# A chunked delta-rule scan in fp32: both directions in lockstep, transposes between the inversion's products

## The chip, the cores and the metric

The kernel runs on one core of a Trainium2 chip, as one program. The metric is the time of one execution on the device in microseconds, less is better. Arithmetic is fp32; the engines named below are PE (matrix products), PEld (its weight loads), DVE (vector), ACT (scalar), POOL (GpSimd) and SP, whose queue issues the DMAs.

## The reference, cut to what matters

A two-layer backbone: an RWKV-7 mixer, an MLP, a Fourier mixer, an MLP, over 1024 latent tokens of 1024 channels with a prefix of 256 context tokens. The change touches the mixer's scan, which runs for 16 heads of 64 channels and for two directions over 256 + 1024 tokens:

```python
def step(s, inp):
    w_t, k_t, v_t, a_t, b_t = inp[:5]
    sa = jnp.einsum('bhvk,bhk->bhv', s, a_t)
    s = s * w_t[:, :, None, :] + sa[..., None] * b_t[:, :, None, :] + v_t[..., None] * k_t[:, :, None, :]
    y = jnp.einsum('bhvk,bhk->bhv', s, inp[5]) if with_out else None
    return s, y
```

`s` is a 64x64 state per head and direction. Direction 1 runs over the tokens in reverse. The context's outputs are not needed, its final states are where the latent scans start.

## The kernel before, in words

A first phase makes the streams of the scan and writes them to DRAM, scaled by running products of the decays. The scan then takes 64 tokens at a time: 20 steps, the first 4 of context, each for both directions `d`. Within a step the 64 updates are solved at once, as a triangular system: the strictly triangular matrix of a head is cut into two halves of 32 tokens, the diagonal 32x32 blocks are inverted, and the second half is solved after the first. Two heads share a tile (`hh`, on partitions 0 to 63 and 64 to 127), eight pairs `q` lie side by side.

One step in `scan_step`, by the lines of the profile: `mms` (L945) multiplies the streams of the chunk with each other; ACT (L954, L958) and DVE (L961, L966) evacuate that with signs and masks; L975 transposes the stream `bk` (32 transposes, 16 a direction, written together), L979 evacuates them. `scan_invert` inverts all 64 blocks of the step at once on DVE (L1094 to L1138), in a doubling scheme whose last rung is L1121 to L1124, and then joins 16x16 blocks on PE with two products of 16 groups of four 32x32 matmuls (L1145 and L1156). Then for each direction by itself: the state `t` is decayed into `sv` on DVE in two halves (L1001) and into `st` on POOL (L1004); `x_mm` (L1019) makes the right-hand sides; ACT copies a half (L1026); `u_mm` (L1031) applies the inverse of the first half; ACT copies (L1036); `o_mm` (L1044) carries it into the second half; again copy, `u_mm`, copies; `s_mm` (L1056) and L1062 make the new state, L1072 and L1076 the output, L1082 copies it and a DMA stores it. A matmul in fp32 is two records in the profile, a transpose one.

The order on each engine is set by a planner (`Plan.emit`) before anything runs. It holds for every operation a duration, an engine or a choice of engines (`flex`), its dependencies and its PSUM banks, and takes the operation that can start first by its own estimate, ties by the length of what hangs on it. It also models the clock of PE by ticks of 3.413 us, from the `load` given with each product, and where it sees PE wait for a bank it puts in dummy 128x128 matmuls (L1814, "fills"). On the chip each engine then works strictly in that order. The loads of the scan go through SP's queue in plan order and wait there for their ring slots (four for `bk`, six for `L`, three for `sv`). Banks 0 to 3 hold L945 and the transposes, bank 4 the inversion, banks 5 to 7 the chain of the state. Beside the scan, 160 loads of a modulation matrix with a DVE pass each (L885, L886) are spread over steps 3 to 18.

## Time and profile before

| | before |
|---|---|
| median of 3 runs | 3099.05 us (3092.76 to 3102.13) |
| profiled execution | 3100.86 us, span 3099.1 us |
| mean granted PE clock | 0.930 |
| PE, DVE, ACT, POOL busy | 2905.6, 1902.2, 998.6, 535.9 us |
| the 20 inversions, by their last copy (L1160) | 673.8 to 1304.1 us |

Busy time is the union of an engine's instructions, so in-order engines are often busy with something that nobody waits for. "Issue" among the releasers of a wait means that nothing in the profile shows what ended it. The granted clock is the share of PE's full clock.

### The profile page before, as it was taken

What the parts mean: (1) busy time and instruction counts of PE and PEld (TensorE: products, weight loads), DVE (VectorE), ACT (ScalarE), POOL (GpSimd) and SP (SyncE); (2) the same over time, 40 slices, a digit from 0 to 9 for tenths busy, and PEclk for the clock granted to TensorE, in tenths of its full rate; (3) what the DMA queues carried; (4) which work ended last, traced back from release to release, by engine and by line L of the source; (5) the groups of instructions that cost most, each with busy time, mean ns of one, the idle gap of its engine ahead of it and who ended that gap; (6) DMA issues with size and microseconds to landing.
All of it is one profiled execution on the core that took longest, in us unless ns stands there. A gap on an engine that the chain in (4) does not pass through costs nothing.

```text
span 3099.1 us, 65486 instructions
## 1 busy us (share of the span) xinstructions
PE 2905.6 (94%) x27884; PEld 2258.6 (73%) x27884; DVE 1902.2 (61%) x3316; ACT 998.6 (32%) x1943; POOL 535.9 (17%) x449
## 2 busy tenths in 40 slices
PE   9999989988878888799999999999899999999998
PEld 5443446477777777789878888888798788888887
DVE  5397785457666666687566556545877544554456
ACT  4363554245444555443211211111322111111121
POOL 2163452201001000111111001100331110111010
PEclk9999999967777877799999999999989999999999
DMA  9266476623344444553132323211031111111111
GB/s 276 86 182 174 136 194 177 160 66 100 107 128 124 134 117 120 158 186 102 58 109 92 96 89 107 70 48 47 8 120 42 52 47 38 55 48 48 41 45 55
DMA packets 297299, 313.03 MB, mean 101 GB/s; under 512 B 81024, under 2 KB 212224, under 8 KB 297008
## 3 DMA queue, kind: packets, MB, share of 16 engines
q1 hardware_dynamic: 295648, 304.01, 33.1%
q8 instruction: 219, 3.59, 0.5%
q0 software_dynamic: 1360, 4.84, 0.5%
q14 instruction: 72, 0.59, 0.1%
HBM read 246.38 MB, written 62.39 MB: 100 GB/s over the span
## 4 chain that ended last, share of the span: by engine, by line
PE 71%; DVE 10%; DMA 6%; issue 3%; ACT 2%; POOL 0%; SPq 0%; DVEq 0%; ACTq 0%; POOLq 0%
PE ps L364 16%; PE ps L366 16%; PE ps L365 16%; PE ps L617 4%; DMA sW<-in_k_mwt_dram 3%; PE ps L620 3%; PE ps L1031 2%; PE ps L945 2%; PE ps L1056 1%; PE ps L1044 1%; PE ps L1019 1%; PE ps L1072 1%; PE ps L1076 1%; DVE bU L456 1%; PE ps L1156 1%
## 5 line engine op out<-in xcount | busy, mean ns | idle before, releaser
L364 PE MATMUL ps<-rU,rU 128*128 128x512 f32 (+3 forms) x2632 | 979.0, 372 | 9.8 <-DVE rX L1509 8.0
L366 PE MATMUL ps<-rU,rU 128*128 128x512 f32 (+3 forms) x2632 | 974.9, 370 | 6.5 <-DVE rU L1239 3.7
L365 PE MATMUL ps<-rU,rU 128*128 128x512 f32 (+3 forms) x2632 | 974.6, 370 | 0.0
L364 PEld LDWEIGHTS ps<-rU,rU 128*128 128x128 f32 x2632 | 500.5, 190 | 105.1 <-DVE rX L1509 9.1
L366 PEld LDWEIGHTS ps<-rU,rU 128*128 128x128 f32 x2632 | 500.6, 190 | 98.0 <-DVE rU L1239 5.2
L365 PEld LDWEIGHTS ps<-rU,rU 128*128 128x128 f32 x2632 | 500.6, 190 | 89.5
L1509 DVE SCALAR_TENSOR_TENSOR rX<-ps,mods,rX 128x512 f32<-128x512 f32 (+1 forms) x528 | 375.6, 730 | 122.3 <-PE ps L366 120.5
L1239 POOL TENSOR_TENSOR rU<-rW,rU 128x512 fp32r<-128x512 f32 x73 | 117.2, 1611 | 1018.8 <-PE ps L366 521.7
L1488 ACT ACTIVATE rS<-ps 128x512 f32<-128x512 f32 x122 | 73.1, 599 | 680.9 <-PE ps L366 680.2
L620 PE MATMUL ps<-bU,bU 128*128 128x512 f32 (+1 forms) x544 | 237.5, 573 | 2.6 <-ACT bS L423 1.9
L423 ACT CAST rU<-rW 128x512 fp32r<-128x512 f32 x160 | 96.3, 616 | 346.8 <-PE ps L366 251.3
L423 DVE CAST rU<-rW 128x512 fp32r<-128x512 f32 x116 | 56.8, 500 | 221.0 <-PE ps L365 210.1
L423 DVE CAST rU<-rS 128x512 fp32r<-128x512 f32 (+1 forms) x99 | 46.9, 479 | 229.5 <-ACT rS L1491 203.4
L1239 DVE TENSOR_TENSOR rU<-rW,rU 128x512 fp32r<-128x512 f32 x201 | 175.5, 893 | 19.7 <-ACT rU L423 19.3
L620 PEld LDWEIGHTS ps<-bU,bU 128*128 128x128 f32 x544 | 100.2, 193 | 109.1 <-issue 98.2
L617 PE MATMUL ps<-bU,bU 128*128 128x512 f32 x304 | 141.7, 607 | 0.0
L945 PE MATMUL ps<-sU,sX 64*128 64x128 f32 (+1 forms) x1280 | 125.5, 353 | 16.8 <-DVE sU L961 7.8
L945 PEld LDWEIGHTS ps<-sU,sX 64*128 64x128 f32 x1280 | 111.9, 255 | 25.2 <-issue 11.7
L961 DVE TENSOR_TENSOR sU<-ps,sW 64x256 f32<-64x256 f32 x160 | 67.5, 422 | 85.7 <-ACT sX L954 44.8
L1239 POOL TENSOR_TENSOR rU<-rS,rU 128x512 fp32r<-128x512 f32 x39 | 60.7, 1559 | 280.8 <-ACT rU L423 125.9
L1036 ACT COPY sU<-ps 32x512 f32<-32x512 f32 x160 | 92.3, 577 | 43.4 <-PE ps L1031 40.2
L617 PEld LDWEIGHTS ps<-bU,bU 128*128 128x128 f32 x304 | 56.6, 192 | 61.6 <-issue 57.8
(268 smaller groups left out, 3899.2 us busy)
## 6 DMA issues: line engine op xcount, KB each, us to landing
rW<-in_mlp_w_dram SPq DMA_DIRECT2D x256, 256.0 KB
rW<-in_k_mwt_dram SPq DMA_DIRECT2D x96, 256.0 KB
sX<-s_bk SPq DMA_DIRECT2D x40, 512.0 KB
s_ar<-bU SPq DMA_DIRECT2D x32, 512.0 KB
sU<-s_ar SPq DMA_DIRECT2D x64, 256.0 KB
sW<-in_k_mwt_dram SPq DMA_DIRECT2D x64, 256.0 KB
bU<-in_rk_wk_dram SPq DMA_DIRECT2D x48, 256.0 KB
bU<-in_rk_wv_dram SPq DMA_DIRECT2D x48, 256.0 KB
```

Source lines behind the costliest of these rows:

```text
L364: nc.tensor.matmul(out, w[0], x[0], start=start, stop=False)
L365: nc.tensor.matmul(out, w[0], x[1], start=False, stop=False)
L366: nc.tensor.matmul(out, w[1], x[0], start=False, stop=stop)
L423: self.nc.scalar.copy(out, src) if e == "act" else self.engines[e].tensor_copy(out, src)
L617: fn = lambda B=B, x=x, w=w, ms=ms, kt=kt: nc.tensor.matmul(B.tile, x[:, ms], w, start=kt == 0, stop=kt == KT - 1)
L620: fn = lambda B=B, x=x, w=w, ms=ms, kt=kt, n=n: nc.tensor.matmul(B.tile[:, :n], w[:, ms], x[:, :n], start=kt == 0, stop=kt == KT - 1)
L945: nc.tensor.matmul(BB[hh].tile[:, j * P : j * P + nr], bk[HR[hh], q, :], L[hh][HR[hh], q, :nr], start=True, stop=True)
L961: plan.add("dve", 0.41, lambda bv=bv, ro=ro, hh=hh, q4=q4, d=d, L=L: nc.vector.tensor_tensor(L[hh][ro, q4, 0:C], bv()[ro, :, 0:C], self.ma ...
L1036: plan.add("act", 0.58, lambda sv=sv, hh=hh, rows=rows, U=U: nc.scalar.copy(sv[rows[hh], hh].rearrange("p q c -> p (q c)"), U.tile[rows[hh ...
L1239: plan.flex({"dve": n / 960 + 0.07, "pool": n / 440 + 0.08}, lambda e: self.engines[e].tensor_tensor(out(1), src(), f32(out(0)), ALU.subtr ...
L1488: plan.flex({"act": 0.53, "dve": 0.6}, lambda e, B=B, s=s: nc.scalar.activation(s.tile[:, :512], B.tile, AF.Relu) if e == "act" else nc.ve ...
L1509: plan.add("dve", n / 960 + 0.12, lambda B=B, m=m, n=n, xs=xs: nc.vector.scalar_tensor_tensor(xs(), B.tile[:, :n], self.mod(layer, 5, m), ...
```

## The change

Both directions now go through the chain together. `x_mm` of both writes two banks, one for each half `z`, with the partitions chosen such that direction 1 has its token halves swapped (`RZ`; the first phase writes `bk` accordingly, and the mask is rolled): so each `u_mm` and the `o_mm` work on all four 32x32 diagonal quadrants of the array, once for both directions. `xs` is copied once for both. The copies behind `u_mm`, and those of the decayed state, may go to ACT or DVE. The state is decayed once, on DVE, into `st`, and copied from there into `sv`; POOL's decay is gone. The transposes have no block of their own; one is issued behind each group of four products in `scan_invert`, the direction 0's in the first product, direction 1's in the second, each product cut in two halves for the planner. In the doubling, the intermediate `pa` is stored transposed and the four operations are planned one by one. The product that reads the state for the output and the one that adds the chunk's own part are planned apart.

```diff
@@ -812,7 +812,9 @@
-        self.flex_tt(n, bk[:, :ng, 0], gv(ta), p1[:, :ng], ALU.mult, [kta, kp1], [(kbk, 0)])
+        hv = lambda ap: ap.rearrange("p g (w t) -> p g w t", w=2)
+        self.flex_tt(n, hv(bk[:, :ng, 0])[:, :, flip], hv(gv(ta)), hv(p1[:, :ng]), ALU.mult, [kta, kp1], [(kbk, 0)])
...
@@ -901,8 +903,8 @@
-        R0 = [slice(hh * 64, hh * 64 + 32) for hh in range(2)]
-        R1 = [slice(hh * 64 + 32, hh * 64 + 64) for hh in range(2)]
+        RZ = [[[slice(hh * 64 + 32 * (d ^ z), hh * 64 + 32 * (d ^ z) + 32) for hh in range(2)] for d in range(2)] for z in range(2)]
...
@@ -967,19 +969,7 @@
-            BB = [self.plan.bank(range(4)) for _ in range(2)]
-            def trs(BB=BB, bk=bk):
-                for q in range(8):
-                    for hh, rs in enumerate(HR):
-                        nc.tensor.transpose(BB[hh].tile[:, q * C : (q + 1) * C], bk[rs, q, :], self.ident[rs, rs])
-            plan.add("pe", 1.1, trs, [kb], [*BB, (kt_, 0), (kt_, 1)], load=0.5)
-            for hh, B in enumerate(BB):
-                plan.add("act", 0.68, lambda B=B, bkt=bkt, hh=hh: nc.scalar.activation(
-                    bkt[:, hh].rearrange("p x t -> p (x t)"), B.tile, AF.Copy, scale=self.sgn[:, hh : hh + 1]),
-                    [B, self.ksgn], [(kt_, hh)], B)
-        tt, kT = self.scan_invert(mab, kM)
+        tt, kT = self.scan_invert(mab, kM, S)
@@ -996,56 +986,59 @@
                 plan.add("pool", 0.5, lambda st=st: nc.gpsimd.memset(st, 0.0), (), [ks])
             else:
                 t, kt0, pcs = self.state[d]
+                plan.add("dve", 0.76, lambda d=d, t=t, st=st: nc.vector.tensor_tensor(
+                    st, t, self.pcs[:, d, :, i - 1 : i].broadcast_to([P, 8, C]), ALU.mult), [kt0, *pcs], [ks])
                 for hh in range(2):
-                    rs = HR[hh]
-                    plan.add(("dve", "dve")[hh], 0.78, lambda rs=rs, hh=hh, d=d, t=t, sv=sv: (nc.vector, nc.vector)[hh].tensor_tensor(
-                        sv[rs, hh], t[rs], self.pcs[rs, d, :, i - 1 : i].broadcast_to([64, 8, C]), ALU.mult),
-                        [kt0, *pcs], [(kv, "s0", hh), (kv, "s1", hh)])
-                plan.add("pool", 1.22, lambda d=d, t=t, st=st: nc.gpsimd.tensor_tensor(
-                    st, t, self.pcs[:, d, :, i - 1 : i].broadcast_to([P, 8, C]), ALU.mult), [kt0, *pcs], [ks])
+                    plan.flex({"act": 0.58, "dve": 0.45}, lambda e, hh=hh, sv=sv, st=st: self.copy_on(e, sv[HR[hh], hh], st[HR[hh]]),
+                              [ks], [(kv, "s0", hh), (kv, "s1", hh)])
+        XB = [self.plan.bank(range(5, 8)) for _ in range(2)]
+        four = [(d, hh) for hh in range(2) for d in range(2)]
+        vkeys = [[(E["kv"], z, hh) for z in ("s0", "s1", "v") for hh in range(2)] for E in S]
         for d in range(2):
             E = S[d]
...
+            def x_mm(d=d, L=E["L"], sv=E["sv"]):
                 for q in range(8):
                     for z in range(2):
                         for hh in range(2):
+                            nc.tensor.matmul(XB[z].tile[RZ[z][d][hh], q * C : (q + 1) * C], L[hh][:, q, 32 * z : 32 * z + 32],
                                              sv[:, hh, q, :], start=z == 0 or q == 0, stop=z == 0)
 
+            kL = E["kL"]
+            lall = [(kL, "a", 0), (kL, "a", 1)] + [(kL, "k", hh, h4) for hh in range(2) for h4 in range(2)]
+            self.at = plan.add("pe", 0.6, x_mm, lall + vkeys[d], [(XB[0], d), (XB[1], d)], load=1.0)
+        for z in range(2):
+            xs, kx = slot("xs")
+            plan.flex({"act": 0.58}, lambda e, z=z, xs=xs: self.copy_on(e, xs, XB[z].tile), [(XB[z], 0), (XB[z], 1)], [kx], XB[z])
+            U = self.plan.bank(range(5, 8))
+            def u_mm(xs=xs, U=U, z=z):
+                for q in range(8):
+                    for d, hh in four:
+                        rs = RZ[z][d][hh]
+                        nc.tensor.matmul(U.tile[rs, q * C : (q + 1) * C], tt[rs, d * 8 + q, :], xs[rs, q * C : (q + 1) * C],
+                                         start=True, stop=True)
+            plan.add("pe", 0.65, u_mm, [kx, kT], [U], U, load=0.25)
+            for d, hh in four:
+                rs, sv, kv = RZ[z][d][hh], S[d]["sv"], S[d]["kv"]
+                plan.flex({"act": 0.58, "dve": 0.68}, lambda e, rs=rs, sv=sv, hh=hh, U=U: self.copy_on(
+                    e, sv[rs, hh].rearrange("p q c -> p (q c)"), U.tile[rs]), [U], [(kv, f"s{z}", hh)], U)
+            if z:
+                continue
+            def o_mm():
+                for q in range(8):
+                    for d, hh in four:
+                        nc.tensor.matmul(XB[1].tile[RZ[1][d][hh], q * C : (q + 1) * C], mab[RZ[0][d][hh], 1, d * 8 + q, :],
+                                         S[d]["sv"][RZ[0][d][hh], hh, q, :], start=False, stop=q == 7)
+            plan.add("pe", 0.65, o_mm, [(E["kv"], "s0", hh) for E in S for hh in range(2)] + [
+                (kM, d, hh, h4, 0) for d in range(2) for hh in range(2) for h4 in range(2)], [(XB[1], 0), (XB[1], 1)], XB[1], load=0.25)
+        for d in range(2):
+            E = S[d]
+            L, kL, sv, kv, vall = E["L"], E["kL"], E["sv"], E["kv"], vkeys[d]
             if i < NCH - 1:
                 bkt, kt_ = E["bkt"], E["kt"]
                 B = self.plan.bank(range(5,8))
...
@@ -1066,24 +1059,26 @@
-                plan.add("pe", 2.1, y_mm, vall + [E["ks"], (kL, "a", 0), (kL, "a", 1)]
-                         + [(k2, hh, h4) for hh in range(2) for h4 in range(2)], [Y], Y, load=0.85)
+                plan.add("pe", 0.95, r_mm, vall + [E["ks"], (kL, "a", 0), (kL, "a", 1)], [Y], Y, load=0.5)
+                plan.add("pe", 1.05, y_mm, vall + [(k2, hh, h4) for hh in range(2) for h4 in range(2)], [Y], Y, load=1.0)
...
@@ -1116,14 +1111,16 @@
+                p = at(ta, 0, [(n * n, n), (n, n), (1, n)])
+                long = {4: 0.26, 8: 1.03}[n]
+                plan.add("dve", long, lambda o=o, p=p, z=z: nc.vector.tensor_tensor(
+                    p, at(m, o + z, [(16, n), (0, n), (1, n)]), at(x, o, [(0, n), (1, n), (16, n)]), ALU.mult), [km, kx], [kta])
+                plan.add("dve", long * 0.7 + 0.04, lambda p=p, pa=pa: nc.vector.tensor_reduce(at(pa, 0, [(1, n), (n, n)]), p, AX.X, ALU.add),
+                         [kta], [kpa])
+                plan.add("dve", long * 0.7 + 0.04, lambda o=o, p=p, z=z, pa=pa: nc.vector.tensor_tensor(
+                    p, at(x, o + z + n, [(16, n), (0, n), (1, n)]), at(pa, 0, [(0, n), (n, n), (1, n)]), ALU.mult), [kpa, kx], [kta])
+                plan.add("dve", long * 0.7 + 0.04, lambda o=o, p=p, z=z: nc.vector.tensor_reduce(
+                    at(x, o + z, [(16, n), (1, n)]), p, AX.X, ALU.add), [kta], [kx])
@@ -1139,25 +1136,44 @@
         Q = [slice(32 * g, 32 * g + 32) for g in range(4)]
         H, T = self.plan.bank((4,)), self.plan.bank((4,))
-        def h_mm():
-            for y in range(16):
+        HR = [slice(0, 64), slice(64, 128)]
+        TB = [[self.plan.bank(range(4)) for _ in range(2)] for _ in range(2)]
+        def turn(d, y):
+            nc.tensor.transpose(TB[d][y % 2].tile[:, y // 2 * C : (y // 2 + 1) * C], S[d]["bk"][HR[y % 2], y // 2, :], self.ident[HR[y % 2], HR[y % 2]])
+        def turned(d):
+            bkt, kt_ = S[d]["bkt"], S[d]["kt"]
+            for hh, B in enumerate(TB[d]):
+                plan.add("act", 0.68, lambda B=B, hh=hh: nc.scalar.activation(
+                    bkt[:, hh].rearrange("p x t -> p (x t)"), B.tile, AF.Copy, scale=self.sgn[:, hh : hh + 1]),
+                    [(B, 0), (B, 1), self.ksgn], [(kt_, hh)])
+        def h_mm(w):
+            for y in range(8 * w, 8 * w + 8):
                 for q in Q:
                     nc.tensor.matmul(H.tile[q, y * 16 : y * 16 + 16], mab[q, 0, y, :], xt[q, y, 0:16], start=True, stop=True)
-        plan.add("pe", 3.0, h_mm, [kxt, *ms], [H], H, load=0.15)
+                turn(0, y)
+        for w in range(2):
+            plan.add("pe", 1.3, lambda w=w: h_mm(w), [kxt, *ms, S[0]["kb"]], [(H, w), *[(X, w) for X in TB[0]]], load=0.45)
         hp, khp = slot("hp")
         plan.add("dve", 0.48, lambda: nc.vector.scalar_tensor_tensor(
             hp[:, :, 0:16], H.tile[:, :256].rearrange("p (y s) -> p y s", y=16), hi,
-            self.cst[:, 0:16].rearrange("p (e c) -> p e c", e=1).broadcast_to([P, 16, 16]), ALU.mult, ALU.add), [H, self.kcst], [khp], H)
-        def t_mm():
-            for y in range(16):
-                for q, o in zip(Q, (0, 64, 32, 96)):
-                    nc.tensor.matmul(T.tile[o : o + 32, y * 32 : y * 32 + 32], hp[q, y, :], xd[q, y, :], start=True, stop=True)
-        plan.add("pe", 1.9, t_mm, [khp, kxd], [T], T, load=0.45)
+            self.cst[:, 0:16].rearrange("p (e c) -> p e c", e=1).broadcast_to([P, 16, 16]), ALU.mult, ALU.add), [(H, 0), (H, 1), self.kcst], [khp])
+        turned(0)
+        def t_mm(w):
+            for y in range(8 * w, 8 * w + 8):
+                for q in Q:
+                    nc.tensor.matmul(T.tile[q, y * 32 : y * 32 + 32], hp[q, y, :], xd[q, y, :], start=True, stop=True)
+                turn(1, y)
+        for w in range(2):
+            plan.add("pe", 1.3, lambda w=w: t_mm(w), [khp, kxd, S[1]["kb"]], [(T, w), *[(X, w) for X in TB[1]]], load=0.55)
+        turned(1)
         tt, kT = slot("tt")
-        plan.add("act", 0.58, lambda: nc.scalar.copy(tt.rearrange("p y t -> p (y t)"), T.tile), [T], [kT], T)
+        plan.add("act", 0.58, lambda: nc.scalar.copy(tt.rearrange("p y t -> p (y t)"), T.tile), [(T, 0), (T, 1)], [kT])
         return tt, kT
```

Three places in PE's order. The first is a step in the middle of the latent scan, before: L1145 and L1156 are the inversion's two products, L945 the products of the next chunk, L1031 and L1044 `u_mm` and `o_mm`, L1056 `s_mm`.

```order
L945 MATMUL ps_90<-sU_190,sX_203 128x128
L1031 MATMUL ps_95<-sU_172,sS_163 32x64 x16
L1031 MATMUL ps_97<-sU_173,sS_163 32x64 x16
L1156 MATMUL ps_94<-sU_175,sU_174 32x32 x64
L1044 MATMUL ps_96<-sU_188,sX_202 32x64 x16
L1056 MATMUL ps_97<-sU_189,sU_177 64x64 x16
L1072 MATMUL ps_96<-sU_170,sU_201 64x64
```

Each product of the inversion is one run of 64 matmuls. The transposes L975 stand a little behind in the same order, in runs of 16, here after a `u_mm`:

```order
L1031 MATMUL ps_95<-sU_172,sS_163 32x64 x16
L975 MATMUL ps_91<-ident,sX_203 128x64
L975 MATMUL ps_93<-ident,sX_203 128x64
L975 MATMUL ps_91<-ident,sX_203 128x64
L975 MATMUL ps_93<-ident,sX_203 128x64
```

Now the second product is L1169, the transposes are L1143 and `x_mm`, ahead of them, L1005:

```order
L1005 MATMUL ps_96<-sU_187,sU_191 32x64
L1005 MATMUL ps_96<-sU_187,sU_190 32x64
L1169 MATMUL ps_94<-sU_175,sU_174 32x32 x4
L1143 MATMUL ps_93<-ident,sX_203 128x64
L1169 MATMUL ps_94<-sU_175,sU_174 32x32 x4
L1143 MATMUL ps_92<-ident,sX_203 128x64
L1169 MATMUL ps_94<-sU_175,sU_174 32x32 x4
L1143 MATMUL ps_93<-ident,sX_203 128x64
L1169 MATMUL ps_94<-sU_175,sU_174 32x32 x4
```

This alternation goes on for all 16 groups of each product, so 32 times a step. Behind it in the same step follow L947 (the chunk's products), L1020 (`u_mm`) and L1034 (`o_mm`):

```order
L947 MATMUL ps_90<-sU_197,sX_203 128x128
L947 MATMUL ps_91<-sU_196,sX_203 128x128
L1020 MATMUL ps_95<-sU_173,sW_155 32x64 x32
L1034 MATMUL ps_96<-sU_188,sX_202 32x64
L1034 MATMUL ps_96<-sU_187,sX_202 32x64
```

One `u_mm` of 32 matmuls stands where there were two of 16, and `o_mm`, which reads the copies of its result, comes next on PE. Behind the second `u_mm` of that step stand fills (L1830) and the output's product L1065:

```order
L947 MATMUL ps_92<-sU_194,sX_203 128x128
L1020 MATMUL ps_97<-sU_173,sW_155 32x64 x32
L1830 MATMUL ps_95<-ident 128x128 x6
L1065 MATMUL ps_95<-sU_170,sU_193 64x64
L1065 MATMUL ps_95<-sU_170,sU_192 64x64
```

The whole program has 212 fills before and 392 now.

56 lines of the change are left out of this document (10 added, 46 removed).

## Prediction

> **What bounds the kernel now.** I read the page for the places where the clock sags, then one window over the scan, then its PE groups, then single starts.
>
> ```profile
> span 3099.1 us, 65486 instructions
> PEclk9999999967777877799999999999989999999999
> ```
>
> Each of the 40 digits stands for 77.5 us; the dip to 6, 7 and 8 lies between about 620 and 1310 us. This is the scan. Its steps are counted on the state addition, two for each of 19 steps:
>
> ```profile
> L1062 DVE TENSOR_TENSOR sU<-ps,sU x38: 653/691/693, 697.6 to 1307.5; 128x512 f32<-128x512 f32 x38
> ```
>
> Nearly 18.5 step lengths lie between the first and the last: (1307.5 - 697.6) / 18.5 = 33 us; with 33.2 the 600 us of the next window hold 18.1 steps. Its columns are the length, then busy time and count on PE, the weight loads, DVE, ACT and POOL, then the granted clock and DMA.
>
> ```profile
> 650.00:700.00 50.00, 43.36 (x1088) 40.09 (x1081) 36.45 (x84) 24.30 (x58) 4.25 (x5) 0.57 0.18 55
> 700.00:1300.00 600.00, 499.43 (x14828) 456.00 (x14827) 405.32 (x897) 300.40 (x637) 59.56 (x57) 0.77 0.42 122
> ```
>
> PE is busy for 499.4 of 600 us, 27.6 us a step, at a granted clock of 0.77; DVE for 22.4, ACT for 16.6. PE bounds the scan, with 5.6 us a step idle. What it does, and why it is idle, stands in its groups in that window (busy and mean ns, then idle time ahead of the group and what ended it):
>
> ```profile
> L945 PE MATMUL ps<-sU,sX 64*128 64x128 f32 (+1 forms) x1056 | 100.4, 347 | 6.6 <-DMA sU<-s_ar 2.7 <-DMA sX<-s_bk 2.4 <-DVE sU L961 0.9
> L1031 PE MATMUL ps<-sU,sW 32*32 32x64 f32 x1536 | 66.1, 258 | 7.7 <-ACT sU L1026 3.7 <-issue 3.6
> L1044 PE MATMUL ps<-sU,sX 32*32 32x64 f32 x1152 | 57.0, 260 | 9.1 <-ACT sU L1036 7.0 <-issue 1.3 <-ACT sU L1026 0.8
> L1056 PE MATMUL ps<-sU,sU 128*64 128x64 f32 x1152 | 53.3, 261 | 0.7 <-ACT sU L1036 0.7
> L1019 PE MATMUL ps<-sU,sU 128*32 128x64 f32 x2304 | 48.1, 237 | 9.7 <-issue 8.4 <-DVE sU L1001 1.0 <-DMA sU<-s_v 0.2
> L1072 PE MATMUL ps<-sU,sU 64*64 64x64 f32 x928 | 42.1, 254 | 2.5 <-issue 2.5
> L1076 PE MATMUL ps<-sU,sU 128*64 128x64 f32 x928 | 39.9, 250 | 0.0
> L1031 PE MATMUL ps<-sU,sS 32*32 32x64 f32 x786 | 32.1, 250 | 6.8 <-issue 5.7 <-ACT sU L1026 1.0
> L975 PE MATMUL ps<-ident,sX 64*128 64x64 f32 x576 | 31.3, 260 | 10.3 <-DVE sU L966 10.1
> L1156 PE MATMUL ps<-sU,sU 32*32 32x32 f32 x2216 | 28.7, 205 | 21.6 <-issue 14.3 <-DVE sU L1149 7.3
> L1145 PE MATMUL ps<-sU,sX 32*32 32x16 f32 x2176 | 28.3, 187 | 25.6 <-issue 23.6 <-DVE sU L1138 2.1
> L1814 PE MATMUL ps<-ident 128*128 128x128 f32 x18 | 3.1, 311 | 0.0
> ```
>
> "Issue" alone is 59.4 us, 3.3 us a step: PE waits for nothing that shows, most in the two products of the inversion (L1145, L1156), which use up instructions fastest. Real waits are 41 us, 2.3 a step.
>
> **The change part by part**, per step, at the mix of clocks of these rows.
>
> *Lockstep.* u_mm (L1031) and o_mm (L1044) came as 32 records on two quadrants of the array; now 64 records run on four. Two quadrants took 98.2 us for 2322 records, 1.35 us per 32; o_mm 57.0 / 36 = 1.58. The nearest row for 64 records of 64 columns on four parts of the array is x_mm (L1019): 48.1 / 36 = 1.34 us. So u_mm goes from 4 x 1.35 to 2 x 1.34, o_mm from 2 x 1.58 to 1.34: **-4.5 us**. Bounds: no overlap of the added quadrants would make it 0.
>
> *Transposes dealt out.* The 32 transposes (L975) used to stand in two runs of 16. Now one stands behind each of the 32 groups of four 32x32 products. They use a 64x128 part of the array, the products 32x32 parts. What such a change of shape costs shows in the starts on both sides of one: the last records of the old shape, then the first of the new. Three at full clock, two at half (the row behind them has the clock, 0.50, around the fourth):
>
> ```profile
> 1031.23 0.22 PE L975 MATMUL ps<-ident,sX 64*128 64x64 f32 x2
> 1031.39 0.25 PE L1156 MATMUL ps<-sU,sU 32*32 32x32 f32 x6
> ```
> ```profile
> 730.83 0.17 PE L1145 MATMUL ps<-sU,sX 32*32 32x16 f32 x1
> 730.94 0.39 PE L945 MATMUL ps<-sU,sX 64*128 64x128 f32 x2
> ```
> ```profile
> 1067.96 0.19 PE L1156 MATMUL ps<-sU,sU 32*32 32x32 f32 x1
> 1068.09 0.38 PE L945 MATMUL ps<-sU,sX 64*128 64x128 f32 x2
> ```
> ```profile
> 813.22 0.32 PE L975 MATMUL ps<-ident,sX 64*128 64x64 f32 x2
> 813.47 0.32 PE L1044 MATMUL ps<-sU,sX 32*32 32x64 f32 x2
> ```
> ```profile
> 836.88 0.22 PE L1145 MATMUL ps<-sU,sX 32*32 32x16 f32 x2
> 837.03 0.58 PE L945 MATMUL ps<-sU,sX 64*128 64x128 f32 x2
> ```
>
> ```profile
> 813.00:814.00 1.00, 1.00 (x21) 0.88 (x20) 0.97 (x2) 0.96 (x3) 0.00 (x0) 0.50 0.13 49
> ```
>
> From a transpose to a product 0.16 us pass at full clock and 0.25 at half; from a product to the shape of the transposes (L945 has it) 0.11 to 0.13 and 0.15. Without a change of shape:
>
> ```profile
> 1031.39 1.27 PE L1156 MATMUL ps<-sU,sU 32*32 32x32 f32 x127
> 1097.11 2.08 PE L1156 MATMUL ps<-sU,sU 32*32 32x32 f32 x128
> ```
>
> that is, less the 0.2 or 0.3 us that the last one takes, 8.4 ns a record, or 14 at half clock: the 8 records of one group span some 0.06 or 0.11 us. A round of group, transpose and group again is therefore 0.06 + 0.12 + 0.16 = 0.34 us, or 0.51 at half clock, and 32 rounds are 10.9 or 16.3. A product of 16 rounds lasts 5.4 us and computes little; I let two thirds run at full clock: 12.7. The three lines cost (31.3 + 28.7 + 28.3) / 18.1 = 4.9 now: **+7.8 us**. Bounds: +6.0 and +11.4; and if a lone transpose pays no change of shape, a round is one group and one transpose, about 0.10 us, and the term is -1.7.
>
> The loads of the transposes' input stand on SP's queue, which waits for them:
>
> ```profile
> SPq L910 <- PE ps L975: 130.7, 24, 17.7
> ```
>
> The ring has four slots, two steps. Now a slot comes free with its product, up to a step later, and the load behind it, with all that SP issues next, moves by as much. L945 needs that load one to two steps later, and today waits 5 us in all for loads: 0, but a load that comes late would hold PE at once.
>
> *Overlap.* The lines above add up to 530 us against 499.4 of PE's busy time, 1.7 us a step of overlap; much of it is products of the same 32x32 shape from different lines running into each other, which transposes in between stop. I take **+0.8** (0 to 1.7).
>
> *Issue.* Nine matmuls in 0.34 us use up instructions several times slower than before, so the 37.9 us of L1145 and L1156 should go: **-2.1** (to 0). The 10.1 us in which transposes waited for L966 go too: **-0.5**.
>
> *New waits.* In the order o_mm follows u_mm with nothing, or one block of eight products, between; it waits for four copies, two each on ACT and DVE. One is
>
> ```profile
> L1036 ACT COPY sU<-ps 32x512 f32<-32x512 f32 x144 | 83.0, 577 | 39.1 <-PE ps L1031 36.1
> ```
>
> so two take 1.2 us, and everything behind o_mm on PE waits with it. Before, work of the other direction often stood there. **+0.9** (0 to 1.5). The order also has 180 more fill matmuls, 9 a step; at 3.1 us for 18 records (9 fills) they cost 3.1 if PE were never idle there, nothing if always. Most stand behind the second u_mm, whose copies PE must await anyway: **+0.8**.
>
> *State and inversion.* On DVE, 76 decays of half the partitions go and 38 of all partitions come, with copies from the result:
>
> ```profile
> L1001 DVE TENSOR_TENSOR sU<-sU,pcs 64x512 f32<-64x512 f32 x71 | 69.9, 984 | 1.7
> L1123 DVE TENSOR_TENSOR sS<-sS,sS 128x64 f32<-128x64 f32 (+1 forms) x51 | 27.8, 544 | 1.8
> ```
>
> Two of 0.98 per direction become one of 0.98 and two copies side by side of about 0.58: 0.4 us shorter, and a hop longer. The new form is unmeasured; between the addition's 0.69 and two old decays, it can win or lose 0.5 us. POOL's own decay only fed a later matmul. L1123 can gain from its new strides, at most 0.4 us on its long form. DVE had 11 us a step to spare, and the inversion runs ahead of its use: 0. The swapped halves in the first phase multiply the same elements: 0.
>
> *Sum:* -4.5 + 7.8 + 0.8 - 2.1 - 0.5 + 0.9 + 0.8 = +3.2 us a step. A longer PE also covers waits for DMA and DVE that stand open today, among them
>
> ```profile
> DVE sW L886 <- DMA sW<-in_k_mwt_dram: 57.1, 12, 10.8
> ```
>
> of which I let 0.6 us a step disappear. **+2.6 us a step, 20 steps, +52 us.** The profiled execution took 3100.9 us, 1.8 above the span and 1.8 above the median of the runs (3099.05): 3100.9 + 52 = **3153 us**. Its own range, from 10.9 and 14.5 us for the rounds with the smaller terms at their ends, is 3110 to 3205.
>
> **The rivals.** (1) *A lone transpose pays no change of shape*, because its weights are loaded under the products. Then the sum is -4.5 - 1.7 - 2.1 - 0.5 + 0.9 + 0.8 = -7.1 us a step. DVE, with its 405 us and the 57 us wait in the window (25.6 us a step), then stands close behind, so I count half: -3.5, 3031 us. For it: the loads overlap elsewhere. Against it: every change of shape quoted pays. It decides if a round takes under about 0.2 us.
>
> (2) *The clock.* PE's records cover 87% of 650 to 700 us, yet the clock was 0.57: being busy is not enough. A round fills little of the array, so all rounds may run at half clock: 16.3 instead of 12.7, +3.6 more a step, 3225 us.
>
> (3) *Full clock throughout*, as PE no longer pauses in the products and has fills for its gaps. At full clock the groups follow each other like this:
>
> ```profile
> 1028.58 1.15 PE L1072 MATMUL ps<-sU,sU 64*64 64x64 f32 x32
> 1029.66 0.51 PE L1076 MATMUL ps<-sU,sU 128*64 128x64 f32 x10
> ```
> ```profile
> 1105.43 1.10 PE L1019 MATMUL ps<-sU,sU 128*32 128x64 f32 x64
> 1106.46 1.30 PE L1145 MATMUL ps<-sU,sX 32*32 32x16 f32 x118
> ```
> ```profile
> 1068.09 1.16 PE L945 MATMUL ps<-sU,sX 64*128 64x128 f32 x16
> ```
>
> x_mm, u_mm and o_mm are five groups of 1.03, state and output six of 1.08, L945 four of 1.16, the rounds 10.9: 27.2. With 4 us of waits (2.3 + 1.2 of issue + 0.9 + 0.8, less 0.6 and 0.5) that is 31.2, or -2.0 a step: 3061 us. The Trainium skill, page "TensorE: Matmul & The Clock Gate", Part 1, states that about 3.4 us of sustained activity release the full clock; read as mere busyness that is this rival. The row of 650 to 700 us disagrees, so the chance is small. The same page's Part 4 says that transposes do not count as busy for this gate, which is (2); no row here isolates it.
>
> (4) *The work is hidden.* PE's idle 5.6 us a step take the extra in: about 3100 us. Against it: 3.3 of them are "issue", which further work does not fill.
>
> **How the numbers follow.** Forecast 0.55; (1) 0.13; (2) 0.12; (3) 0.07; (4) 0.13. From these: slower 0.55 + 0.12 + 0.03 of (4) = 0.70, same 0.08 of (4), faster 0.13 + 0.07 + 0.02 = 0.22; the bound is 0.3%, 9 us, about what a measurement can tell. The range 3060 to 3230 takes in all but (1), which is 0.13, and the tails.
>
> **What would show it.** In the new trace each round, from one transpose to the next, lasts 0.3 to 0.5 us; L1155, L1169 and L1143 together hold PE for 11 to 14 us of a step; their "issue" idle is nearly gone; L1020 and L1034 fall to about 4 us a step; steps are near 36 us. PE stays over 85% busy. I am wrong if rounds take 0.2 us or less, if u_mm on four quadrants takes as long as two separate ones, or if the granted clock moves by more than 0.1.

## The result and the profile after

The changed kernel takes 3209.39 us (median of 4 runs, 3203.03 to 3212.48), the kernel before 3099.2 in the same runs: a ratio of 1.0356, with a 95% interval of 1.0332 to 1.0379. It is slower by 110 us, where the forecast was 3153, slower by 54.

From the page of the changed kernel, the span and the granted clock in 40 slices, each now 80 us long:

```profile
span 3210.4 us, 66076 instructions
PEclk9999999966788777789999999999989999999999
```

The dip of the scan is as deep as before and longer. The state addition, by its line, and the same window as before (length, then busy time and count on PE, weight loads, DVE, ACT and POOL, then granted clock and DMA):

```profile
L1055 DVE TENSOR_TENSOR sU<-ps,sU x38: 641/681/694, 706.5 to 1408.4; 128x512 f32<-128x512 f32 x38
```
```profile
700.00:1300.00 600.00, 563.03 (x12981) 461.00 (x12973) 330.00 (x816) 241.23 (x522) 12.34 (x23) 0.74 0.35 103
700.00:1250.00 550.00, 516.49 (x11974) 424.16 (x11969) 301.60 (x737) 223.91 (x486) 11.86 (x22) 0.75 0.35 103
```

A step takes (1408.4 - 706.5) / 18.5 = 37.9 us, against 33.0: 5.0 more, and 20 steps are 100 of the 110 us. PE is busy for 563.03 / 600 x 37.9 = 35.6 us of a step (27.4 before) and idle for 2.3 (5.5). So 8.2 us of work came and 3.2 of idle time went. Where the work is, by PE's groups in the window of 600 us (busy and mean ns, then idle time ahead and what ended it):

```profile
L1143 PE MATMUL ps<-ident,sX 64*128 64x64 f32 x491 | 162.8, 332 | 0.0
...
L1169 PE MATMUL ps<-sU,sU 32*32 32x32 f32 x1936 | 75.3, 234 | 10.1 <-DVE sU L1161 10.1
L1155 PE MATMUL ps<-sU,sX 32*32 32x16 f32 x1992 | 69.3, 204 | 0.0
...
L1830 PE MATMUL ps<-ident 128*128 128x128 f32 x210 | 33.7, 305 | 2.6 <-DVE sU L968 2.6
...
L1034 PE MATMUL ps<-sU,sX 32*32 32x64 f32 x960 | 29.5, 235 | 13.3 <-ACT sU L423 8.4 <-DVE sU L423 4.5
L1020 PE MATMUL ps<-sU,sW 32*32 32x64 f32 x1280 | 28.3, 250 | 1.9 <-issue 1.9
L1020 PE MATMUL ps<-sU,sS 32*32 32x64 f32 x640 | 13.2, 241 | 0.0
```

The transposes (L1143) have become PE's costliest group. The issue waits of the two products (37.9 us before) are gone. Lines overlap, so their busy times don't add up. Counted from each matmul's start to the next one's (to its own end where a gap follows), transposes and both products hold PE for 14.6 us of a step, against 4.5 before. `u_mm` and `o_mm` fell from 155.2 us of line time in 18.2 steps, 8.5 a step, to 71.0 in 15.8, 4.5.

Rounds can be read off the timeline (start, length, line). Two windows, and behind them the clock around each:

```profile
1006.34 0.25 PE L1155 MATMUL ps<-sU,sX 32*32 32x16 f32 x8
1006.52 0.27 PE L1143 MATMUL ps<-ident,sX 64*128 64x64 f32 x1
1006.72 0.25 PE L1155 MATMUL ps<-sU,sX 32*32 32x16 f32 x8
1006.90 0.27 PE L1143 MATMUL ps<-ident,sX 64*128 64x64 f32 x1
...
1011.17 0.36 PE L1143 MATMUL ps<-ident,sX 64*128 64x64 f32 x1
1011.46 0.30 PE L1155 MATMUL ps<-sU,sX 32*32 32x16 f32 x8
1011.70 0.36 PE L1143 MATMUL ps<-ident,sX 64*128 64x64 f32 x1
```
```profile
1006.00:1007.00 1.00, 1.00 (x32) 0.81 (x28) 1.00 (x2) 0.24 (x2) 0.00 (x0) 1.00 0.21 51
1011.00:1012.00 1.00, 1.00 (x21) 0.69 (x20) 0.00 (x0) 0.00 (x0) 0.00 (x0) 0.50 0.17 49
```

From transpose to transpose 0.38 us pass at full clock and 0.53 at half. Over all 563 rounds that lie in one clock the medians are 0.38 (first product) and 0.40 (second), 0.53 and 0.55, and 359 of them (64%) run at half clock.

### The profile page after: what moved, and what is told of

Its sections match the earlier page's. It is cut to its first block, busy times and chain, and to the rows that moved or that the text cites. A ratio compares the mean times of both kernels' runs of the same rounds, so it can differ in the third digit from the quotient of the medians.

```text
span 3210.4 us, 66076 instructions
## 1 busy us (share of the span) xinstructions
PE 3085.2 (96%) x28244; PEld 2358.3 (73%) x28244; DVE 1874.1 (58%) x3344; ACT 977.0 (30%) x1903; POOL 496.3 (15%) x421
## 3 DMA queue, kind: packets, MB, share of 16 engines
q1 hardware_dynamic: 295648, 304.01, 31.6%
## 4 chain that ended last, share of the span: by engine, by line
PE 80%; DVE 10%; ACT 3%; DMA 3%; issue 2%; POOL 0%; SPq 0%; DVEq 0%; ACTq 0%; POOLq 0%
PE ps L364 16%; PE ps L366 16%; PE ps L365 16%; PE ps L620 5%; PE ps L1143 5%; PE ps L617 4%; PE ps L1169 2%; PE ps L947 2%; PE ps L1830 2%; PE ps L1155 2%; PE ps L1020 2%; PE ps L1005 2%; ACT sU L423 1%; DVE bU L456 1%; PE ps L574 1%
## 5 line engine op out<-in xcount | busy, mean ns | idle before, releaser
L1143 PE MATMUL ps<-ident,sX 64*128 64x64 f32 x640 | 212.1, 331 | 0.0
L620 PEld LDWEIGHTS ps<-bU,bU 128*128 128x128 f32 x544 | 99.6, 192 | 106.2 <-issue 96.7
L947 PE MATMUL ps<-sU,sX 64*128 64x128 f32 (+1 forms) x1280 | 119.4, 336 | 9.0 <-DVE sU L963 5.8
L433 POOL TENSOR_SCALAR sU<-sS,sS 128x256 f32<-128x256 f32 x29 | 15.2, 531 | 717.8 <-DVE sS L1122 639.8
L1143 PEld LDWEIGHTS ps<-ident,sX 64*128 64x128 f32 x640 | 104.2, 163 | 29.3 <-issue 0.3
L1830 PE MATMUL ps<-ident 128*128 128x128 f32 x784 | 113.0, 300 | 7.4 <-DMA ident<-in_k_ident_dram 2.7
```

Of the source, the lines that this page charges most:

```text
L620: fn = lambda B=B, x=x, w=w, ms=ms, kt=kt, n=n: nc.tensor.matmul(B.tile[:, :n], w[:, ms], x[:, :n], start=kt == 0, stop=kt == KT - 1)
L947: nc.tensor.matmul(BB[hh].tile[:, j * P : j * P + nr], bk[HR[hh], q, :], L[hh][HR[hh], q, :nr], start=True, stop=True)
L1143: nc.tensor.transpose(TB[d][y % 2].tile[:, y // 2 * C : (y // 2 + 1) * C], S[d]["bk"][HR[y % 2], y // 2, :], self.ident[HR[y % 2], HR[y % 2]])
L1830: self.plan.fill = lambda t: nc.tensor.matmul(t[:, :P], self.ident, self.ident, start=True, stop=True)
```

## Experiments

### The two halves of the change

**Transposes back in blocks of 16**, each product planned in one piece with its old duration, and everything else of the change kept:

```diff
-                turn(0, y)
...
-                turn(1, y)
...
+            plan.add("pe", 1.1, trs, [kb], [*BB, (kt_, 0), (kt_, 1)], load=0.5)
```

> The changed kernel, with the transposes in a block of 16 a direction ahead of the inversion, as they stood before, and the rest of the change kept. Theory A (the alternation of shapes costs the time): the three lines of products and transposes hold PE for about 15 us a step in the changed kernel and 4.5 before; as blocks they give back some 10.4 us a step, and 2.0 us of issue waits and 0.5 of other waits return: -8 us a step, 20 steps, about 3050 us, under the kernel before. Rival L (lockstep itself, with its waits and fills, costs the time): at most 60 us come back, 3150 us or more.

Measured: 3052.46 us, ratio to before 0.9842 (0.9813 to 0.987), as theory A has it. So with lockstep in place, dealing out costs 3209.4 - 3052.5 = 157 us, and the rest of the change gains 47. Its steps and window:

```profile
L1067 DVE TENSOR_TENSOR sU<-ps,sU x38: 647/683/692, 696.8 to 1260.3; 128x512 f32<-128x512 f32 x38
```
```profile
700.00:1250.00 550.00, 424.94 (x14892) 385.25 (x14882) 372.27 (x913) 274.49 (x588) 13.34 (x24) 0.85 0.44 131
```

A step is 30.5 us, 23.5 busy and 6.9 idle. PE is busy for 77% of the window here at a clock of 0.85, and for 94% in the changed kernel at 0.75: busier, and granted less.

**Dealing out alone**, on the kernel before:

```diff
-            plan.add("pe", 1.1, trs, [kb], [*BB, (kt_, 0), (kt_, 1)], load=0.5)
...
+                turn(0, y)
...
+                turn(1, y)
```

> The kernel before, with its transposes dealt out between the inversion's products as the change does, and nothing else of it. A: +10.4 us of PE a step less 2.6 of waits, +8 us a step, about 3255 us, slower than the whole change. L: within 30 us of the kernel before.

Measured: 3207.35 us, 1.0344 (1.0311 to 1.0377), 107 us slower: the way of A, but 48 us short of its 3255. Lockstep and the two DVE parts are worth nothing once the transposes are dealt out (3207.35 and 3209.39), and 47 us where they are not. The window of this kernel:

```profile
700.00:1250.00 550.00, 534.31 (x11918) 446.62 (x11918) 322.26 (x732) 242.37 (x521) 52.45 (x47) 0.75 0.35 103
```

A step is 37.5 us, with 1.1 idle; transposes and both products hold PE for 14.7, as in the changed kernel. From here to the changed kernel `u_mm` and `o_mm` fall from 7.2 to 4.5 us a step by their lines, while the fills rise from 0.5 to 2.1 and the idle time from 1.1 to 2.3. What lockstep saves comes back in these two.

### The number of changes of shape

The changed kernel, with the transposes collected behind every second, fourth, eighth or last group (`g` stands for 2, 4, 8 or 16):

```diff
-                turn(0, y)
+                if y % g == g - 1:
+                    for u in range(y - g + 1, y + 1):
+                        turn(0, u)
```

> The changed kernel with the transposes dealt out by twos, 32 changes of shape a step. If the change of shape is the price, the step from 64 to 16 of them (115 us, 2.4 us for each one less in a step) puts this one half way down and a third more: 3209 - 32 x 2.4 = 3132 us. If single transposes are dear for another reason (their weights cannot be loaded ahead), pairs take most of it away: 3105 or less.

> The changed kernel, with the transposes dealt out by fours: four groups of products, then four transposes; 16 changes of shape a step in place of 64, everything else the same. A, priced by the change of shape: three quarters of the 10.4 us go, about 1 us of issue waits returns, -6.8 us a step, about 3075 us. If a transpose among products costs by its number and not by the changes of shape, or L: within 20 us of 3209.

> Dealt out by eights, 8 changes of shape a step. Price per change: 3094 - 8 x 2.4 = 3075 us. Rival: with longer runs of products PE uses up its instructions faster than they come, and the issue waits take back what the changes give: 3090 to 3100.

> All 16 transposes of a direction in one run behind the product they were dealt into, 4 changes of shape a step, the planner's numbers those of the change. Price per change: 3065 us. Rival (issue waits): 3090 to 3100. If the place of the block matters (behind a product here, ahead of the inversion in the block version with 3052 us), it differs from that by more than 15 us.

| transposes in a run | us | step, us | PE busy | PE idle | of it issue | clock |
|---|---|---|---|---|---|---|
| 1 (changed) | 3209.39 | 37.9 | 35.6 | 2.3 | 0.1 | 0.75 |
| 2 | 3106.49 | 32.5 | 28.0 | 4.4 | 1.4 | 0.84 |
| 4 | 3094.32 | 32.2 | 26.0 | 6.2 | 2.7 | 0.83 |
| 8 | 3087.56 | 32.0 | 24.8 | 7.2 | 3.3 | 0.85 |
| 16 | 3084.59 | 31.6 | 24.1 | 7.6 | 3.6 | 0.86 |
| blocks of their own | 3052.46 | 30.5 | 23.5 | 6.9 | 4.9 | 0.85 |

(PE's columns are shares of the 550 us from 700 to 1250, times the step; the clock is the granted one of that window.) PE's work falls with every halving, as a price per change of shape says. The time falls by 103 us with the first halving and by 22 with the other three together. From pairs on, most of what PE saves comes back as idle time, and two thirds of that rise is "issue". By these rows, that is why runs of four, eight and sixteen stayed 13 to 20 us above the price per change.

Pairs came out 26 us below it, next to the 3105 of the rival that single transposes are dear for another reason. The window and the starts of that kernel speak against this reason:

```profile
700.00:1250.00 550.00, 475.08 (x14028) 403.88 (x14020) 353.40 (x875) 260.81 (x564) 14.60 (x27) 0.84 0.41 124
```
```profile
1047.26 0.28 PE L1143 MATMUL ps<-ident,sX 64*128 64x64 f32 x2
1047.47 0.31 PE L1155 MATMUL ps<-sU,sX 32*32 32x16 f32 x16
```

The second transpose of a pair starts 3 ns behind the first (median), and the products start 0.20 us (full clock) or 0.30 us (half) behind the second, as they do behind a lone one (behind four or more it is 0.15 and 0.24). So a change of shape has the same price in both kernels. What pairs changed besides is the clock: 0.84 in place of 0.75 in the window, and 43% of the rounds at half clock in place of 64%. That this is what made pairs better than expected is argued, not shown.

The last two rows are 32 us apart, over the 15 that were to show that the place of the block matters. They differ in the place (behind a product, or ahead of the inversion) and in the planning of the products; which of the two counts was not separated. So 125 of the 157 us go with the number of changes alone.

### Shape, or any second source?

**Four small products for each transpose.** No change of shape, but 16 records a round in place of 9:

```diff
-            nc.tensor.transpose(TB[d][y % 2].tile[:, cols], S[d]["bk"][HR[y % 2], y // 2, :], ident)
+            for c in range(4):
+                r = Q[y % 2 * 2 + c // 2]
+                nc.tensor.matmul(TB[d][y % 2].tile[Q[c], cols], S[d]["bk"][r, y // 2, Q[c]], ident, ...)
```

> The changed kernel with each lone 64x128 transpose replaced by four products of the inversion's own 32x32 shape (64 columns each, with the identity), in the same place; they read half of the rows each, so half of the transposed stream is left out. Theory A (a lone transpose is dear because it changes the shape of the array's use twice): without a change of shape a round is 8 records of 8.4 ns and 8 of at most 21 ns, 0.24 us at full clock against 0.39 in the changed kernel, and some 0.35 against 0.54 at half clock; 32 rounds save 5 to 6 us a step, so about 3105 us (3080 to 3140). Rival B (the cost is in alternating between two sources, or in the number of instructions, which rises from 9 to 16 a round): no gain, 3190 us or more.

Measured: 3182.34 us, 1.0264 (1.0232 to 1.0295). By the time, neither side has it: it lies above theory A's range and 8 us below rival B's. The window and groups tell more:

```profile
700.00:1300.00 600.00, 456.66 (x17169) 406.81 (x17162) 339.64 (x832) 252.99 (x547) 13.36 (x25) 0.78 0.36 108
700.00:1250.00 550.00, 417.11 (x15781) 371.51 (x15776) 310.86 (x765) 229.48 (x495) 11.94 (x22) 0.78 0.37 109
```
```profile
L1145 PE MATMUL ps<-ident,sX 32*32 32x64 f32 x4096 | 119.0, 269 | 33.3 <-issue 33.3
...
L1171 PE MATMUL ps<-sU,sU 32*32 32x32 f32 x2048 | 59.9, 232 | 39.7 <-issue 30.5 <-DVE sU L1163 9.1
L1157 PE MATMUL ps<-sU,sX 32*32 32x16 f32 x2048 | 52.2, 196 | 26.5 <-issue 26.4
```

PE's busy time fell from 563 to 457 us, with a third more records. But 90.2 us of "issue" stand ahead of these three lines, where the changed kernel has none. The theory was right for PE; the time went into waits that have no visible releaser.

**One small product for each transpose**, 10 records a round:

```diff
-            nc.tensor.transpose(TB[d][y % 2].tile[:, cols], S[d]["bk"][HR[y % 2], y // 2, :], ident)
+            r, c = Q[y % 2 * 2], Q[y // 2 % 4]
+            nc.tensor.matmul(TB[d][y % 2].tile[c, cols], S[d]["bk"][r, y // 2, c], ident, start=True, stop=True)
...
-                    bkt[:, hh] ..., B.tile, AF.Copy, scale=self.sgn[:, hh : hh + 1]), ...
+                    bkt[:, hh], S[d]["bk"][:, :, hh * C : hh * C + C], AF.Copy, scale=0.0), ...
```

The evacuations on ACT now read the stream itself and scale it by 0, so this kernel leaves the transposed stream out.

> The changed kernel with each lone 64x128 transpose replaced by one product of the inversion's own 32x32 shape (64 columns, with the identity): 10 records a round, as good as the 9 before, and no change of shape. The evacuations write zeros into the transposed stream, so it is left out and the state only decays. Theory A (the price of a lone transpose is the change of shape, and the kernel with four small products a round was held by the supply of instructions): PE busy falls below 470 of 600 us, issue waits come to 3 to 5 us a step, 3080 to 3125 us. Rival B (any second source between the groups costs as much): rounds stay at 0.39 and 0.54 us, 3180 us or more.

Measured: 3125.55 us, 1.0085 (1.0062 to 1.0108), 84 us less than the changed kernel and 0.6 us above theory A's range, whose two other signs hold (PE busy for 466.6 of 600 us, 4.0 us of issue a step). Its window, and both ends of one product with its 16 rounds:

```profile
700.00:1250.00 550.00, 429.55 (x14482) 388.00 (x14473) 356.82 (x874) 255.49 (x564) 10.11 (x21) 0.83 0.41 120
...
1030.00:1032.00 2.00, 2.00 (x156) 2.00 (x156) 1.37 (x3) 1.20 (x4) 0.00 (x0) 0.54 0.04 8
```
```profile
1029.94 0.25 PE L1156 MATMUL ps<-sU,sX 32*32 32x16 f32 x8
1030.02 0.22 PE L1144 MATMUL ps<-ident,sX 32*32 32x64 f32 x1
...
1032.10 0.31 PE L1144 MATMUL ps<-ident,sX 32*32 32x64 f32 x1
1032.10 0.26 PE L1156 MATMUL ps<-sU,sX 32*32 32x16 f32 x2
```

16 rounds in 2.2 us, 0.14 us each, mostly at half clock (0.54), against 0.53 with the transpose: more instructions, a second source, and no stop between groups. A step has 25.8 us of PE's work in place of 35.6. Half of those 9.8 us came back as waits: idle time is 7.2 in place of 2.3, 4.0 of it "issue".

This kernel takes away the change of shape and the transpose at once. The kernel before keeps them apart: it goes from 64x128 products (L945) straight to 32x32 products, with no transpose. Here is one at full clock:

```profile
1120.44 0.27 PE L945 MATMUL ps<-sU,sX 64*128 64x128 f32 x1
1120.64 0.26 PE L1156 MATMUL ps<-sU,sU 32*32 32x32 f32 x8
```

From start to start 0.20 us pass in each of 20 such changes at full clock (700 to 1300 us), and 0.35 in each of 13 at half, against 7 ns (median) from one 32x32 product to the next. So the change of shape is what costs; it is shown. The Trainium skill, page "TensorEngine Tiling (Array Packing)", section "Key Properties", states that a change of the tiling mode drains TensorE while tiles of one mode work independently of each other. The two kernels agree; here it is 0.2 us (full clock) to 0.3 (half) behind each lone transpose.

### What the rest of the change gains, and from what

The prediction put the two DVE parts, the state's decay and the inversion's rungs, at 0. Each is undone on the kernel with blocks, with its planning (and for the decay, POOL's product comes back), then both, and then they are put alone on the kernel before:

```diff
-                plan.add("dve", 0.76, ... st, t, self.pcs[:, ...] ...)
-                for hh in range(2):
-                    plan.flex({"act": 0.58, "dve": 0.45}, ... sv[HR[hh], hh], st[HR[hh]] ...)
+                for hh in range(2):
+                    plan.add("dve", 0.78, ... sv[rs, hh], t[rs], self.pcs[rs, ...] ...)
+                plan.add("pool", 1.22, ... st, t, self.pcs[:, ...] ...)
```
```diff
-                ... at(pa, 0, [(1, n), (n, n)]) ... at(pa, 0, [(0, n), (n, n), (1, n)])
+                ... at(pa, 0, [(n, n), (1, n)]) ... at(pa, 0, [(0, n), (1, n), (n, n)])
```

> The lockstep version with the transposes in a block (3052 us), and the state decayed as before: two half decays on DVE straight into the operand, one on POOL, no copies. The prediction costed this part at 0, with 0.5 us a step either way: 3042 to 3062. If the single decay on DVE is a real gain of the change, 3070 or more.

> The kernel with lockstep and the transposes in blocks of 16, with the last rungs of the inversion on DVE as before the change (intermediate not transposed, four operations planned as one). The prediction put this part at 0: 3052 within 10 us. Rival: the inversion's DVE chain stands on the path, and the time is 3065 us or more.

> Lockstep alone: the kernel with lockstep and the transposes in blocks of 16, with the state's old decay and the inversion's old doubling. Theory A (the parts add up: each of the two old parts alone cost 15 us on 3052): 3076 to 3090 us, so lockstep alone gains 10 to 23 us on the kernel before and not the 90 that the prediction's term for PE would give. Rival B (both old parts lengthen the same wait, so that the second costs nothing more): 3068 us or less.

> The kernel before with the two DVE parts alone: the state decayed once, and the inversion's last rungs in the new form; both directions by themselves and the transposes in their blocks, as before. Theory A (the decay stands on the path only in lockstep, where x_mm waited for it 21.6 of 550 us against 1.0 of 600 in the kernel before; without lockstep other work covers it): 3085 to 3105 us, so lockstep and the DVE parts gain only together. Rival B (DVE was short in every order): 3060 us or less, and lockstep adds nothing.

| | us | ratio to before |
|---|---|---|
| lockstep and both DVE parts (blocks) | 3052.46 | 0.9842 (0.9813 to 0.987) |
| without the new decay | 3067.79 | 0.9907 (0.987 to 0.9944) |
| without the new rungs | 3067.77 | 0.9891 (0.9863 to 0.9919) |
| lockstep alone | 3109.29 | 1.0031 (1.001 to 1.0052) |
| both DVE parts alone | 3110.09 | 1.0038 (1.0019 to 1.0056) |

Neither half gains anything by itself, together they gain 47 us. Undoing one DVE part costs 15 us either way, which was the rival's side for the rungs; for the decay it lies between the expected range and the 3070 of a real gain. Both expectations for lockstep alone missed: undoing both costs 57, more than the sum. The DVE parts alone came out as theory A has it, a little above its range. The window of lockstep alone and the groups of PE that wait longest in it:

```profile
700.00:1250.00 550.00, 424.92 (x13896) 382.27 (x13898) 404.69 (x865) 226.47 (x508) 45.75 (x50) 0.85 0.41 120
```
```profile
L947 PE MATMUL ps<-sU,sX 64*128 64x128 f32 (+1 forms) x1024 | 92.4, 330 | 24.9 <-issue 10.3 <-DMA sX<-s_bk 9.5 <-DVE sU L968 4.7
L1019 PE MATMUL ps<-sU,sU 128*32 128x64 f32 x2176 | 55.7, 264 | 29.4 <-DVE sU L1003 21.6 <-issue 7.8
```

A step is 33.3 us, 25.7 busy and 7.6 idle. Lockstep took 1.8 us off PE's busy time and gave 2.1 back as waits. L1019 is `x_mm`, and it waits 21.6 us for the old decay (L1003), which in the kernel before cost 1.0 us of 600: there the other direction's chain ran meanwhile, in lockstep both directions want their decayed state at once (read from the order). DVE is busy for 404.7 of 550 us. The decay by itself, before and in the kernel with blocks (ns: least, median, most):

```profile
L1001 DVE TENSOR_TENSOR sU<-sU,pcs x76: 671/689/1539, 698.3 to 1310.0; 64x512 f32<-64x512 f32 x76
```
```profile
L1001 DVE TENSOR_TENSOR sU<-sU,pcs x38: 673/684/704, 698.0 to 1261.5; 128x512 f32<-128x512 f32 x38
```

Half the partitions take as long as all of them, and often much longer: in the kernel before, 42 of the 76 took 0.67 to 0.69 us and 34 took 0.84 to 1.54. The order of starts tells them apart. Here one half decay starts ahead of POOL's product of the same state (L1004), the other behind it:

```profile
858.14 0.68 DVE L1001 TENSOR_TENSOR sU<-sU,pcs 64x512 f32<-64x512 f32 x1
```
```profile
858.19 1.55 POOL L1004 TENSOR_TENSOR sU<-sU,pcs 128x512 f32<-128x512 f32 x1
```
```profile
858.86 1.44 DVE L1001 TENSOR_TENSOR sU<-sU,pcs 64x512 f32<-64x512 f32 x1
```

The first loses nothing, the second ends 0.55 us behind POOL's product. All 34 long ones began while an operation of POOL was running (33 times L1004) and ended 0.54 to 0.55 us behind it. Of the 42 short ones only one began beside such an operation, 17 ns before that ended; during 18 of them L1004 began, and they took no longer. POOL's product, in turn, took 1.06 us (median) where no decay was running at its start and 1.50 where one was. So of the two, the one that starts second waits. Without POOL's product no decay takes over 0.704. What this alone is worth in time is not shown, since no run moved POOL's product by itself.

### Fills, and the order

The changed kernel and the one with blocks, each without the scan's fill matmuls:

```diff
+            if op["step"] is not None and op["step"] < 19:
+                op["fills"] = 0, blank
```

> The changed kernel without the fill matmuls of the scan (about 9 a step), order otherwise the same. A with the fills as a cost: they hold PE for 2.0 us a step, some 0.8 of it in waits for copies: -24 us, about 3185. Rival: the fills keep the clock of PE up, and without them the granted clock in the scan falls under 0.72 and the time rises to 3220 or more.

> The kernel with lockstep and the transposes in blocks of 16, without the fill matmuls in the scan's steps. Theory A (fills delay PE's work, as in the changed kernel, where leaving them out gave 10 us): 3035 to 3047 us. Rival B (they hold the granted clock up where PE would wait): the clock falls by 0.01 or more and the time is 3055 us or more.

Measured: 3198.88 us (1.0314, 1.0284 to 1.0345) and 3052.53 (0.9847, 0.982 to 0.9875). Fills cost the changed kernel about 10 us, where theory A had 24; PE has only 2.3 us a step idle there. The granted clock of its window is 0.74 without them (0.75 with), so the rival, which wanted less than 0.72, falls. In the kernel with blocks they cost nothing, and the clock stays at 0.85: both its expectations missed.

The planner's durations nearer to the trace, and then fewer and larger transposes:

```diff
-            self.at = plan.add("pe", 0.6, x_mm, ...)
+            self.at = plan.add("pe", 1.05, x_mm, ...)
-            plan.add("pe", 0.65, u_mm, ...)
+            plan.add("pe", 1.05, u_mm, ...)
-            plan.add("pe", 0.65, o_mm, ...)
+            plan.add("pe", 1.05, o_mm, ...)
-        plan.add("pe", 3.0, h_mm, [kxt, *ms], [H], H, load=0.15)
+        plan.add("pe", 1.3, h_mm, [kxt, *ms], [H], H, load=0.1)
-        plan.add("pe", 1.9, t_mm, [khp, kxd], [T], T, load=0.45)
+        plan.add("pe", 1.1, t_mm, [khp, kxd], [T], T, load=0.25)
```
```diff
-                        nc.tensor.transpose(BB[hh].tile[:, ...], bk[rs, q, :], self.ident[rs, rs])
+                    nc.tensor.transpose(BB[q // 4].tile[:, ...], bk[:, q, :], self.ident)
```

> The kernel with lockstep and the transposes in blocks of 16, but with the planner's durations for x_mm, u_mm, o_mm (1.05 us) and the two products of the inversion (1.3 and 1.1 us) near what the trace shows instead of 0.6, 0.65, 3.0 and 1.9. Theory A (part of what lockstep saves on PE is lost in the order): 3030 to 3045 us. Rival B (what it loses is in waits that no order changes, the issue waits first): 3052 within 6.

> The fastest kernel so far (lockstep, blocks, the planner's durations near the measured ones, 3035 us) with 16 transposes of 128x128 in place of 32 of 64x128 a step, evacuated in four pieces a direction in place of two. Theory A (PE's transposes fall from 1.6 to 0.8 us a step, and 16 matmuls with their loads less have to be supplied): 3010 to 3028 us. Rival B (four evacuations on ACT in place of two come later): 3035 us or more.

Measured: 3035.05 us, 0.9793 (0.9764 to 0.9822), for the durations alone, as theory A has it: the fastest kernel, 2.1% below the one before. With the larger transposes on top 3051.24, 0.9843 (0.9821 to 0.9865): theory B. That its four evacuations on ACT are the reason is not shown.

## Why the prediction was right or wrong

**Direction and mechanism were right.** Every lone transpose pays a change of shape (rival 1 falls: rounds are far above 0.2 us), issue waits vanish from the products, and the extra work is not hidden (rival 4 falls). Steps were to be near 36 us and are 37.9; L1155, L1169 and L1143 were to hold PE for 11 to 14 us and hold it for 14.6; L1020 and L1034 fell to 4.5. One argument failed on the way: against rival 4 the prediction says that further work does not fill "issue". It did, from 3.5 to 0.1 us a step. Rival 4 falls because 8.2 us of work met 5.5 us of idle time.

**The failed step is the size of "transposes dealt out".** The term had +7.8 us a step. By the count from starts it is 14.6 - 4.5 = +10.1, and the same without lockstep (14.7). These 2.3 us in 20 steps are 46 of the 56 us by which the forecast was short. Two sizes were off. From transpose to product I took 0.16 and 0.25 us, from the ends of runs of 16; behind a lone transpose the median is 0.20 and 0.29, so rounds are 0.38 to 0.40 and 0.53 to 0.55 in place of 0.34 and 0.51. The kernel before had such a price on show, in its changes from L945 to 32x32 products (0.20 and 0.35). And 64% of the rounds run at half clock, where I let one third. Either by itself makes 32 rounds 1.4 to 1.7 us longer than 12.7 (32 x (2/3 x 0.39 + 1/3 x 0.54) = 14.1, and 32 x (0.36 x 0.34 + 0.64 x 0.51) = 14.4); both together would make 15.6, and the count from starts, which lacks a few records (491 of some 506 transposes), has 14.6. Rival 2 (all rounds at half clock, 3225) had the right direction, and the time is nearer to it than to the forecast. Nothing of rival 3 is seen: the window's clock fell from 0.77 to 0.74 with PE busy for 94% of it.

**The other terms are nearer.** `u_mm` and `o_mm` went from 8.5 to 4.5 by lines, -4.0 for -4.5. Fills take 2.1 us a step of PE, 1.9 more than before, where 0.8 were allowed for, though leaving them out gives only 10 us back. Idle time fell by 3.2, where issue, other waits, new waits and covered waits had -2.1 - 0.5 + 0.9 - 0.6 = -2.3. With dealing out at +10.1 that is +4.8 of the measured +5.0. (The prediction counts 18.1 steps of 33.2 us in its window, where its own division gives 33.0; that moves no term by more than 0.1.)

**The runs do not divide the 110 us in one way.** Dealing out, with what goes along with it, had +7.8 + 0.8 - 2.1 - 0.5 = +6.0 us a step, 120 us. Lockstep, its new waits, fills and covered waits had -4.5 + 0.9 + 0.8 - 0.6 = -3.4, -68 us. With lockstep in place the runs have 157 and -47. Taken the other way, with dealing out first, they have 107 and +2. The prediction added the parts as if each were worth the same beside the other.

**"0" for the DVE parts was wrong where the transposes stand in blocks.** I looked for cover in DVE's 11 us a step to spare. The cover was the other direction's work, and lockstep takes that away. Undoing either part costs 15 us on the kernel with blocks, undoing both 57, and they gain nothing without lockstep. In the changed kernel neither was undone by itself, so there the 0 is not tested. Two decays were counted at a mean of 0.98 us, which mixes 0.69 with up to 1.54.

**Issue** went from the changed kernel as said (-2.1 forecast; from 3.5 to 0.1 us a step over all lines). It is there in every kernel here without the lone transposes (1.4 us a step and more).

## What to carry to other kernels

Before dealing small work between matmuls of another shape, read the starts on both sides of a lone change of shape at both clocks, and multiply by the number of changes: here going from 64 changes a step to 4 gave back 125 us, and pairs already gave 103 of them. Terms that were priced each by itself can be worth something else together, so undo them in both orders. When two chains are put in lockstep, list what each covered for the other, since a term that was free behind the other chain goes onto the path. And where a chip-side wait has no visible releaser, count instructions for each us: in the kernels here, much of what PE's busy time lost came back as such waits.

## What the hardware showed

The waits called "issue" go with the instruction stream. Queue 8 in the page's DMA section carries instructions (packets, MB, share), here for the window 700 to 1250 of the changed kernel and of the one with four small products a round:

```profile
q8 instruction: 93, 1.52, 1.2%
```
```profile
q8 instruction: 123, 2.02, 1.6%
```

By the window's rows PE and its weight loads had 11974 + 11969 and 15781 + 15776 records there: 257 to a packet in both, of 16 KB each. In six kernels I counted the time from one such packet's start to the next: in this window it is never below 3.2 us, and the fastest twentieth lies under 3.4 to 4.0. PE can use up 256 records of the inversion's products in the 1.27 us that the prediction quotes. Of 115 gaps of PE above 0.7 us within one line (in this window of the kernel before, the one with blocks and the one with four small products), 106 ended 1.1 to 1.7 us after a packet had landed; packets start 4.1 to 4.9 us apart there (medians), so about one gap in seven would do so by chance. That the packets' pace (about 13 ns a record at best) makes these waits is a reading that fits all kernels here, the rise from 4.0 to 6.7 us a step between 10 and 16 records a round included. No run changed the pace itself, so it is not shown.

The clock does not follow busy time: 94% busy got 0.75, 77% busy got 0.85. The Trainium skill, page "TensorE: Matmul & The Clock Gate", Part 1, describes the gate by sustained activity; if activity were the busy time of the records, these two windows would stand the other way round. Which share of the array or of the columns the gate counts was not isolated.
